# A two-layer transformer on one core: another way to combine the experts' rows, half a split moved from GpSimd to VectorE, and two modulation sums moved

## The chip, the cores and the metric

The kernel runs on one core of a Trainium2 chip. The metric is the device time of one execution in microseconds (us). The kernel before takes 2536.94 us, the median of three runs (2536.73 to 2538.14). For this kernel 0.2%, 5.07 us, is about what a measurement can tell from no change.

The engines by their short names: PE multiplies matrices, DVE is the vector engine, ACT the scalar engine, POOL is GpSimd. SP issues most DMAs (its queue is SPq); POOL also issues DMAs, among them the gathers by a list of row numbers.

## The reference

512 tokens of 1024 float32 columns pass two layers. In each, `h = x*(1+sc1)+sh1` goes through an attention block of two branches; its result is added to the scaled `x`, multiplied by a gate row, and normalised. Then `h = x*(1+sc2)+sh2` goes through a feed-forward block: dense in layer 0 (1024 to 2816 and back), eight experts in layer 1, of which each token uses the two that its router chose. The rows `sh`, `sc` and `g` are a vector-matrix product with `w_ada`, made once for each layer.

```python
mod = cond @ w_ada[l] + b_ada[l]
sh1, sc1, g1, sh2, sc2, g2 = jnp.split(mod[:, None, :], 6, axis=-1)
...
h = x * (1.0 + sc2) + sh2
f = _swiglu(...) if l % 2 == 0 else _moe(...)
x = _layernorm(DEEPNORM_ALPHA * x + g2 * f, ln2_g[l], ln2_b[l])
```

## The kernel before, in words

**Split products.** Every float32 operand is split into a rounded part (`wh`, `hTh`, by ACT) and the rest (`wl`, `hTl`, a subtraction on DVE or POOL), and each product is three matmuls: high by high, high by low, low by high (`mm3`, L127 to L129). A weight tile is loaded into `ws` by SP (L101), rounded by ACT (L111) and subtracted (L113). There are two `ws` buffers outside the expert stage.

**Order.** The program is written as one list. A planner puts the instructions of each engine in order: of those that its cost model holds ready, the first in the list goes first. On the chip each engine then runs its own list strictly in that order. `order(a, b)` keeps `a` behind `b` on one engine.

**The residual stage** (`residual`, twice with a following `early`): the last 512 columns of the product are finished for token tiles 0 to 3 in turn. DVE adds, takes statistics and normalises each tile (L945 to L947, L311 to L318, L980). After tile 2, `half_h(.., 0)` makes the modulated, turned `hTh` and `hTl` of tiles 0 and 1: for each pair of column blocks, four transposes into one PSUM tile `pt` (two buffers), DVE and ACT scale it into `hmod`, ACT rounds it to `hTh`, and for this half POOL makes all four subtractions `hTl` (L283). Then `early` (`early_ffn` after layer 0's attention, `early_first` after its feed-forward) loads its first weights and multiplies the first half by the column blocks 0 to 4, `half_h(.., 1)` makes the second half after tile 3 is normalised, and `early` goes on.

**The dense feed-forward loop** has 22 steps `f` of two products each. A generator `mod_steps` is resumed four times at the head of each step. For each of seven vectors it loads eight 512 KB pieces `mst` (two buffers), adds them up on DVE into `macc` (L213, L215), lets some resumptions pass (`wait`), sums over the partitions on PE (L222), copies (L225) and turns the result (L229), all with `order` behind the last product or weight split. The same loop writes zeros to the rows of `ybuf` that are kept for overflow, one DMA a step (L1077).

**The experts.** Each token has a place in two of eight slots (336, 320, 128, 128, 64, .. rows); `dst` holds the two row numbers, `gw` the two gates. Slots 0 and 1 run in the big lane, the others in the small lane beside it. A slot's output rows are stored to three buffers `ybuf`, of 512, 256 and 256 columns (`PIECES`). The big lane's last slot (slot 1) makes its output piece by piece: `out_turned`, `turn_back`, store. Then `Final.combine(i)` gathers for each of four token tiles the two rows of each token (eight gathers on POOL, L1681), adds them by their gates (L1683, DVE), and in the last piece normalises and writes the output (L311 to L318, L1689, L1691, L1692, L1694, L1695).

## Time and profile before

| | |
|---|---|
| median of three runs | 2536.94 us (2536.73 to 2538.14) |
| profiled execution, its own time | 2534.31 us |
| its span, first to last instruction | 2532.3 us |
| PE busy | 2431.6 us, 96% of the span |
| DVE, ACT, POOL busy | 70%, 57%, 17% |
| granted PE clock, mean | 0.986 |

Busy shares are averages over stages with different limits. The chain of work that ended last is followed back from the last instruction, at each step to what released it. A row of the time line gives the start, the length, the engine, the line of the kernel, the operation, the tiles written and read, the count of merged instructions, and in brackets the idle time ahead of it and what ended it.

### The profile page before, as it was taken

The numbers are of one execution on the slowest core, as the hardware profiler recorded it, in microseconds if no ns is written. First come the engines' busy times: TensorE is split into PE (matmuls) and PEld (weight loads), VectorE is DVE, ScalarE is ACT, GpSimd is POOL, SyncE is SP. The second block draws the span as 40 slices with busy tenths as digits, with TensorE's granted clock in tenths as the row PEclk, the third lists the DMA queues.
The fourth block names the chain that finished last, engine by engine and source line by source line (L and its number), as shares of the span: only waits on it lengthen the run. The fifth ranks groups of instructions, "written<-read, shape, count | busy, mean of one in ns | idle before, by whom it ended". The sixth has DMA issues, their size and how long they took to land.

```text
span 2532.3 us, 37049 instructions
## 1 busy us (share of the span) xinstructions
PE 2431.6 (96%) x13124; PEld 2077.9 (82%) x13124; DVE 1779.4 (70%) x2788; ACT 1432.8 (57%) x2320; POOL 430.8 (17%) x393
## 2 busy tenths in 40 slices
PE   8999999998999999999999997999999999999994
PEld 6878878787888888888877875888899998999994
DVE  3687876657666235787775356977788888888875
ACT  3577775224222215677763326676676777778761
POOL 1423330001000402333325004300000000000004
PEclk9999999999999999999999998999999999999997
DMA  8322226746866433222226329998999989999993
GB/s 236 90 62 64 75 76 193 220 148 210 273 212 211 150 100 109 78 63 76 73 73 192 100 76 285 316 327 274 318 319 296 320 285 319 333 302 332 293 333 122
DMA packets 453210, 502.20 MB, mean 198 GB/s; under 512 B 19314, under 2 KB 322920, under 8 KB 453016
## 3 DMA queue, kind: packets, MB, share of 16 engines
q1 hardware_dynamic: 437616, 453.64, 56.9%
q0 software_dynamic: 13888, 45.30, 5.1%
q8 instruction: 105, 1.72, 0.3%
q10 hardware_dynamic: 1512, 0.81, 0.1%
q14 instruction: 89, 0.73, 0.1%
HBM read 474.95 MB, written 24.74 MB: 197 GB/s over the span
## 4 chain that ended last, share of the span: by engine, by line
PE 80%; DVE 7%; ACT 4%; DMA 4%; issue 3%; POOL 1%; SPq 0%; ACTq 0%; DVEq 0%; POOLq 0%
PE ps L127 21%; PE ps L128 21%; PE ps L129 21%; PE ps L1373 5%; PE ps L1374 5%; PE pt L445 2%; DMA mst<-in_w_ada 1%; DVE wl L113 1%; PE ps L733 1%; PE ps L734 1%; ACT wh L111 1%; DVE ps L746 1%; ACT ps L742 1%; PE pt L1439 1%; PE ps L716 0%
## 5 line engine op out<-in xcount | busy, mean ns | idle before, releaser
L111 ACT ACTIVATE wh<-ws 128x1024 fp32r<-128x1024 f32 (+3 forms) x786 | 779.1, 1011 | 687.7 <-PE ps L128 343.4
L113 DVE TENSOR_TENSOR wl<-ws,wh 128x1024 fp32r<-128x1024 f32 (+3 forms) x712 | 837.3, 1195 | 365.2 <-ACT wh L111 357.1
L129 PE MATMUL ps<-hTh,wl 128*128 128x512 f32 (+1 forms) x904 | 346.9, 384 | 4.4 <-DVE wl L113 4.4
L127 PE MATMUL ps<-hTh,wh 128*128 128x512 f32 (+1 forms) x904 | 349.7, 387 | 0.1
L128 PE MATMUL ps<-hTl,wh 128*128 128x512 f32 (+1 forms) x904 | 348.7, 386 | 0.8 <-POOL hTl L283 0.8
L129 PE MATMUL ps<-x3h,wl 128*128 128x336 f32 (+1 forms) x704 | 220.5, 313 | 2.2 <-DVE wl L113 2.2
L127 PE MATMUL ps<-x3h,wh 128*128 128x336 f32 (+1 forms) x704 | 221.0, 314 | 0.0
L128 PE MATMUL ps<-x3l,wh 128*128 128x336 f32 (+1 forms) x704 | 219.9, 312 | 0.0
L113 POOL TENSOR_TENSOR wl<-ws,wh 128x1024 fp32r<-128x1024 f32 (+1 forms) x74 | 179.4, 2432 | 212.9 <-ACT wh L111 143.0
L129 PEld LDWEIGHTS ps<-hTh,wl 128*128 128x128 f32 x904 | 171.5, 190 | 36.9 <-DVE wl L113 5.3
L127 PEld LDWEIGHTS ps<-hTh,wh 128*128 128x128 f32 x904 | 171.6, 190 | 36.1 <-issue 3.7
L128 PEld LDWEIGHTS ps<-hTl,wh 128*128 128x128 f32 x904 | 171.4, 190 | 32.6 <-POOL hTl L283 2.1
L1373 PE MATMUL ps<-wh,xes 128*128 128x512 f32 (+1 forms) x384 | 143.3, 379 | 0.0
L1374 PE MATMUL ps<-wl,xes 128*128 128x512 f32 (+1 forms) x384 | 141.4, 374 | 0.0
L127 PEld LDWEIGHTS ps<-x3h,wh 128*128 128x128 f32 x704 | 132.2, 188 | 3.4
L128 PEld LDWEIGHTS ps<-x3l,wh 128*128 128x128 f32 x704 | 132.4, 188 | 3.0
L129 PEld LDWEIGHTS ps<-x3h,wl 128*128 128x128 f32 x704 | 132.1, 188 | 2.7 <-DVE wl L113 2.7
L127 PE MATMUL ps<-wh,hTh 128*128 128x256 f32 (+1 forms) x384 | 116.1, 304 | 1.8 <-DVE dq L520 1.0
L128 PE MATMUL ps<-wl,hTh 128*128 128x256 f32 (+1 forms) x384 | 113.6, 297 | 0.8 <-DVE wl L113 0.8
L129 PE MATMUL ps<-wh,hTl 128*128 128x256 f32 (+1 forms) x384 | 112.7, 295 | 0.0
L124 DVE TENSOR_TENSOR pTl<-pt,pTh 128x512 fp32r<-128x512 f32 x128 | 86.6, 686 | 36.0 <-ACT pTh L123 35.4
L128 PE MATMUL ps<-g3l,wh 128*128 128x336 f32 (+1 forms) x352 | 110.7, 315 | 0.0
(428 smaller groups left out, 5344.5 us busy)
## 6 DMA issues: line engine op xcount, KB each, us to landing
ws<-in_moe_w SPq DMA_DIRECT2D x492, 512.0 KB
ws<-in_w_in SPq DMA_DIRECT2D x94, 512.0 KB
mst<-in_w_ada SPq DMA_DIRECT2D x80, 512.0 KB
ws<-in_ffn_w SPq DMA_DIRECT2D x66, 512.0 KB
ws<-in_moe_w SPq DMA_DIRECT2D x48, 256.0 KB
wa<-in_w_ada SPq DMA_DIRECT2D x16, 512.0 KB
ws<-in_w_br_diff SPq DMA_DIRECT2D x16, 512.0 KB
ws<-in_w_out SPq DMA_DIRECT2D x16, 512.0 KB
```

The lines of the kernel that those rows point to most:

```text
L111: A.activation(h, st, AF.Copy)
L113: i = eng.tensor_tensor(l, st, h, op=OP.subtract)
L124: V.tensor_tensor(l, src, h, op=OP.subtract)
L127: T.matmul(o, ah, bh, start=start, stop=False)
L128: T.matmul(o, ah, bl, start=False, stop=False)
L129: last_mm[0] = T.matmul(o, al, bh, start=False, stop=stop)
L445: T.transpose(pt[:, t * P:(t + 1) * P], tiles[t][:, k * P:(k + 1) * P], ident)
L733: T.matmul(scs[m], q[:, m, tt], k[:, m], start=True, stop=False)
L734: last_mm[0] = T.matmul(scs[m], q[:, m, tt], kl[:, m], start=False, stop=True)
L742: A.activation(e, e, AF.Exp, scale=-1.0, bias=st[:, m:m + 1], accum_out=st[:, 2 + m:3 + m])
L1373: T.matmul(o, xs, wh, start=start, stop=False)
L1374: T.matmul(o, xs, wl, start=False, stop=stop)
```

## The change

Three edits. First, the last 512 columns (pieces 1 and 2). Before the last slot has stored anything there, 16 gathers fetch both rows of each token from `ybuf[1]` and `ybuf[2]`, where the last slot's rows hold zeros written earlier; `others` also works out for each token its row in the last slot (or a row of zeros) and its gate. At the end one row a token is gathered for each of the two pieces. Piece 0 is gathered as before; its adds are interleaved with the last products. Second, in the first half of the modulated input the last two of four subtractions are made from PSUM by DVE, after the second early weight is split. Third, the first two of seven modulation sums wait 7 and 4 resumptions where they waited 5 and 3, and the zeros go out two DMAs a step, 27 in all.

```diff
 def half_h(pool, xtiles, sc, sh, h, l, i, later=None):
+            if later is not None and k2 >= 4:
+                for j in range(2):
+                    k, pj = k2 + j, pt[:, j * 256:j * 256 + 256]
+                    if j == 0:
+                        last_split[0] = V.tensor_scalar(pj, pj, sc[:, k:k + 1], sh[:, k:k + 1], op0=OP.mult, op1=OP.add)
+                    else:
+                        A.activation(pj, pj, AF.Identity, scale=sc[:, k:k + 1], bias=sh[:, k:k + 1])
+                hk = h[:, k2:k2 + 2, tt]
+                mk = pt.rearrange("p (j c) -> p j c", j=2)
+                A.activation(hk, mk, AF.Copy)
+                later.append((l[:, k2:k2 + 2, tt], mk, hk))
+                continue
...
+    def small_parts(later):
+        for o, m, hk in later:
+            i = V.tensor_tensor(o, m, hk, op=OP.subtract)
+            order(i, last_split[0])
+        last_split[0] = i
...
-    zeros = [(y, SLOT_ROWS + i * P) for i in range(N_OVER) for y in ybuf]
+    zeros = [(y, SLOT_ROWS + i * P, P) for i in range(N_OVER) for y in ybuf]
+    zeros += [(y, SLOT[0] + i, min(P, SLOT[1] - i)) for i in range(0, SLOT[1], P) for y in ybuf[1:]]
...
-                 (5, 3, 2, 2, 2, 2, 2))
+                 (7, 4, 2, 2, 2, 2, 2))
...
-        for y, r in zeros[f:f + 1]:
-            SP.dma_start(y[r:r + P, :], zero[:, :y.shape[1]])
+        for y, r, m in zeros[2 * f:2 * f + 2]:
+            SP.dma_start(y[r:r + m, :], zero[:m, :y.shape[1]])
...
                     if nxt is None and i == 1:
                         for _ in gens[1]:
                             pass
-                    yield from out_turned(ew[2], g[1], part, c0, nc_, (FH, FT), False)
+                        fin.others(s)
+                    work = out_turned(ew[2], g[1], part, c0, nc_, (FH, FT), False)
+                    if nxt is None and i == 2:
+                        adds = fin.adds(0, fin.ys[0])
+                        for n in work:
+                            next(adds, None)
+                            yield n
+                        fin.after[0] = last_out[0]
+                        for _ in adds:
+                            pass
+                    else:
+                        yield from work
                     turn_back(part, SLOT[s], c0, nc_, row_stores(s))
-                    if nxt is None and i > 0:
-                        fin.combine(i - 1)
+                    if nxt is None and i == 1:
+                        fin.after[0] = last_out[0]
+                        for j in (1, 2):
+                            for _ in fin.adds(j, fin.ys[j]):
+                                pass
+                        fin.last_place(1)
...
+            late = [self.gathers(1, dst, (("xeh", 4), ("xel", 4))), self.gathers(2, dst, (("xg", 4), ("xg", 4)))]
+            self.ys = [self.gathers(0, dst, (("geh", 5), ("gel", 3)))] + late
...
+        def last_place(self, i):
+            tag = ("hs", "eg")[i - 1]
+            self.ys.append(self.gathers(i, self.row, ((tag, 2), (tag, 2))))
...
+        def end(self):
+            table = exp_table()
+            self.after[0] = last_out[0]
+            for _ in self.adds(1, self.ys[3], self.gate):
+                pass
+            self.last_place(2)
+            for t, _ in enumerate(self.adds(2, self.ys[4], self.gate)):
+                self.norm((t,), 3, table)
```

`early_ffn` calls `small_parts` between its second and third weight, `early_first` between its second and third. `adds` makes the gated adds of one piece, tile by tile, with the statistics; `norm` is the old end of `combine`. The branch for overflowing slots, which keeps the old way in `anew`, is not entered here.

## Rows read from the trace of the kernel before

**Rows 1.** The page: the chain that ended last, by engine.
```profile
PE 80%; DVE 7%; ACT 4%; DMA 4%; issue 3%; POOL 1%; SPq 0%; ACTq 0%; DVEq 0%; POOLq 0%
```

**Rows 2.** Time line of PE and POOL after the first residual.
```profile
583.14 0.58 PE L129 MATMUL ps<-hTh,wl 128*128 128x256 f32 x1 [3.55 <-DVE wl L113]
590.00 0.82 PE L266 MATMUL pt<-ident,u 128*128 128x128 f32 x6
...
579.50 2.49 POOL L283 TENSOR_TENSOR hTl<-hmod,hTh 128x512 fp32r<-128x512 f32 x2
```

**Rows 3.** Time line of DVE in the same stretch.
```profile
579.16 3.92 DVE L113 TENSOR_TENSOR wl<-ws,wh 128x1024 fp32r<-128x1024 f32 x1
584.33 1.21 DVE L113 TENSOR_TENSOR wl<-ws,wh 128x1024 fp32r<-128x1024 f32 x1
586.95 0.81 DVE L980 TENSOR_SCALAR u<-u,bmv 128x1024 f32<-128x1024 f32 x1
```

**Rows 4.** Windows: length, busy PE PEld DVE ACT POOL (count), PEclk, DMA share, GB/s.
```profile
583.00:588.50 5.50, 5.36 (x25) 5.37 (x26) 4.17 (x10) 0.50 (x2) 0.44 (x1) 0.51 0.75 224
588.50:603.00 14.50, 14.49 (x121) 14.13 (x121) 7.06 (x10) 7.07 (x13) 3.62 (x4) 1.00 0.30 88
603.00:619.60 16.60, 16.60 (x74) 13.24 (x72) 12.29 (x13) 6.19 (x9) 0.00 (x0) 1.00 0.93 288
619.60:626.00 6.40, 3.32 (x14) 1.97 (x14) 3.30 (x4) 1.06 (x1) 0.00 (x0) 0.73 0.67 208
965.00:970.00 5.00, 3.58 (x21) 3.35 (x22) 4.94 (x7) 0.60 (x3) 4.66 (x5) 1.00 0.48 159
```

**Rows 5.** Time line of PE and SPq in the feed-forward loop.
```profile
622.88 1.08 PE L222 MATMUL pt<-macc,ones 128*32 128x256 f32 x8 [3.08 <-DVE macc L215]
...
600.54 0.90 SPq L1077 DMA_DIRECT2D ybuf<-zero  x2
612.60 2.12 SPq L210 DMA_DIRECT2D mst<-in_w_ada  x2
```

**Rows 6.** Time line of DVE from the small lane's end to the last instruction.
```profile
2457.40 0.68 DVE L1502 TENSOR_TENSOR ye<-hs,g2row 64x512 f32<-64x512 f32 x1
2484.43 1.01 DVE L1527 SCALAR_TENSOR_TENSOR part<-ps,mcol,part 128x320 f32<-128x320 f32 x2 [4.12 <-PE ps L129]
2486.53 2.09 DVE L1683 SCALAR_TENSOR_TENSOR fu<-yg,r,fu 128x512 f32<-128x512 f32 x3 [0.44 <-DMA yg<-ybuf,r]
2495.81 0.99 DVE L1527 SCALAR_TENSOR_TENSOR part<-ps,mcol,part 128x320 f32<-128x320 f32 x2
2497.86 0.88 DVE L1683 SCALAR_TENSOR_TENSOR fu<-yg,r,fu 128x256 f32<-128x256 f32 x2 [0.67 <-DMA yg<-ybuf,r]
2506.84 0.49 DVE L1683 SCALAR_TENSOR_TENSOR fu<-yg,r,fu 128x256 f32<-128x256 f32 x1 [1.23 <-DMA yg<-ybuf,r]
2524.74 1.29 DVE L1694 SCALAR_TENSOR_TENSOR frows<-frows,bmv 128x1024 f32<-128x1024 f32 x1
```

**Rows 7.** Chain of waits at the end: start, length, what.
```profile
2487.58 4.31 DMA ybuf<-ye
```

**Rows 8.** Time line of POOL: first gather of piece 0, first of piece 2.
```profile
2479.53 1.65 POOL L1681 DMA_INDIRECT yg<-ybuf,r  x1 [22.98 <-DMA ybuf<-ye]
2503.80 1.18 POOL L1681 DMA_INDIRECT yg<-ybuf,r  x1 [1.44 <-issue]
```

**Rows 9.** One line's instructions: count, ns min/median/max, first and last start.
```profile
L1681 POOL DMA_INDIRECT yg<-ybuf,r x24: 943/949/1685, 2479.5 to 2513.5; - x24
```

**Rows 10.** The page: subtraction from PSUM, by DVE.
```profile
L124 DVE TENSOR_TENSOR pTl<-pt,pTh 128x512 fp32r<-128x512 f32 x128 | 86.6, 686 | 36.0 <-ACT pTh L123 35.4
```

**Rows 11.** Time line of DVE and PE after the second residual.
```profile
965.49 1.77 DVE L946 SCALAR_TENSOR_TENSOR u<-u,ftmp 128x512 f32<-128x512 f32 x1
968.73 1.11 DVE L473 TENSOR_SCALAR dgc<-cols 128x8 f32<-128x8 f32 x1
972.02 0.87 PE L266 MATMUL pt<-ident,u 128*128 128x128 f32 x6 [0.41 <-DVE u L980]
```

More of the change, by code (lines that the diff above doesn't have):

```diff
@@ L256, in gate_row, with half_h @@
         return row_tile(pool, "grow", modrow[i:i + 1], "grow")
-    def half_h(pool, xtiles, sc, sh, h, l, i):
+    def half_h(pool, xtiles, sc, sh, h, l, i, later=None):
         tt = slice(i * 256, i * 256 + 256)
@@ L939, in residual @@
         sts = [pool.tile([P, 3, 6], F32, name=nm("bst"), tag="bst", bufs=4) for _ in range(NT)]
+        later = []
         def fin(pz, t, i, c0, n):
@@ L986, in residual @@
                         l = hp.tile([P, KT, S], F32R, name=nm("hTl"), tag="hTl")
-                        half_h(pool, us, *ab, h, l, 0)
+                        half_h(pool, us, *ab, h, l, 0, later)
         if ab is None:
@@ L991, in residual @@
         behind[0] = None
-        e = early(h, l)
+        e = early(h, l, later)
         if EARLY_POOL:
@@ L1014, in build, with early_ffn @@
     ahead_of = {}
-    def early_ffn(h, l):
-        ws = [(f, w, wload([P, KT, P], kview(I[w][0], 0, KT, f * P, P)), psum())
-              for f, w in ((0, "ffn_w1"), (0, "ffn_w3"), (1, "ffn_w1"))]
+    def small_parts(later):
[3 more added lines that the diff above has]
+        last_split[0] = i
+    def early_ffn(h, l, later):
+        ws = []
+        for i, (f, w) in enumerate(((0, "ffn_w1"), (0, "ffn_w3"), (1, "ffn_w1"))):
+            if i == 2:
+                small_parts(later)
+            ws.append((f, w, wload([P, KT, P], kview(I[w][0], 0, KT, f * P, P)), psum()))
         for i, tt in enumerate(halves_of):
@@ L1027, in early_ffn, with early_first @@
         yield
-    def early_first(h, l):
+    def early_first(h, l, later):
         w_in = I["w_in"][1]
@@ L1032, in early_first @@
         pz = [psum() for _ in range(NT)]
+        small_parts(later)
         lat = [wload([P, 2, LAT], kview(w_in, 0, 2, 0, LAT))]
@@ new lines, in gathers @@
+        def gathers(self, i, idx, tags):
+            n = PIECES[i][1]
+            ys = []
+            for tag, k in tags:
+                y = xp.tile([P, k, n], F32, name=nm("yg"), tag=tag, bufs={"xg": XG, "hs": 3, "eg": 2}.get(tag, 1))
+                ys += [y[:, j, :] for j in range(k)]
+            m = idx.shape[2]
+            for t in range(NT):
+                for k in range(m):
+                    G.indirect_dma_start(out=ys[m * t + k], out_offset=None, in_=ybuf[i],
+                                         in_offset=bass.IndirectOffsetOnAxis(ap=idx[:, t, k:k + 1], axis=0))
+            return ys
@@ new lines, in others @@
+        def others(self, s):
+            r, n = starts[s], SLOT[s]
+            here, lt = et([P, NT, 2]), et([P, NT, 2])
+            V.tensor_scalar(here, dstf, r - 0.5, None, op0=OP.is_gt)
+            V.tensor_scalar(lt, dstf, r + n - 0.5, None, op0=OP.is_lt)
+            V.tensor_tensor(here, here, lt, op=OP.mult)
+            V.tensor_scalar(lt, dstf, float(SLOT_ROWS), None, op0=OP.subtract)
+            V.tensor_tensor(lt, lt, here, op=OP.mult)
+            rowf = et([P, NT])
+            V.tensor_reduce(rowf, lt, axis=AX.X, op=OP.add)
+            V.tensor_scalar(rowf, rowf, float(SLOT_ROWS), None, op0=OP.add)
+            self.row = et([P, NT, 1], I32)
+            V.tensor_copy(self.row, rowf.unsqueeze(2))
+            V.tensor_tensor(lt, here, gw.rearrange("p k t -> p t k"), op=OP.mult)
+            self.gate = et([P, 1, NT])
+            V.tensor_reduce(self.gate.rearrange("p o t -> p (o t)"), lt, axis=AX.X, op=OP.add)
+            self.after = [None]
+            late = [self.gathers(1, dst, (("xeh", 4), ("xel", 4))), self.gathers(2, dst, (("xg", 4), ("xg", 4)))]
+            self.ys = [self.gathers(0, dst, (("geh", 5), ("gel", 3)))] + late
@@ new lines, in adds @@
+        def adds(self, i, ys, gate=None):
+            c0, n = PIECES[i]
+            for t in range(NT):
+                uc = self.us[t][:, c0:c0 + n]
+                for k in range(len(ys) // NT):
+                    j = V.scalar_tensor_tensor(uc, ys[len(ys) // NT * t + k], (gw if gate is None else gate)[:, k, t:t + 1],
+                                               uc, op0=OP.mult, op1=OP.add)
+                    if self.after[0] is not None:
+                        order(j, self.after[0])
+                if i == 0 or gate is not None:
+                    V.bn_stats(self.sts[t][:, i, :], uc)
+                yield
@@ new lines, in last_place, with norm @@
+        def last_place(self, i):
+            tag = ("hs", "eg")[i - 1]
+            self.ys.append(self.gathers(i, self.row, ((tag, 2), (tag, 2))))
+        def norm(self, ts, n, table):
+            for t in ts:
+                u = self.us[t]
+                mean, r = ln_stat(xp, self.sts[t][:, :n], table)
+                V.scalar_tensor_tensor(u, u, mean, self.lg, op0=OP.subtract, op1=OP.mult)
+                if t < 2:
+                    A.activation(u, u, AF.Copy, scale=r)
+                    G.tensor_tensor(u, u, self.lb, op=OP.add)
+                else:
+                    V.scalar_tensor_tensor(u, u, r, self.lb, op0=OP.mult, op1=OP.add)
+                SP.dma_start(out[0, t * P:(t + 1) * P, :], u)
@@ new lines, in end, with anew @@
+        def end(self):
[6 more added lines that the diff above has]
+                self.norm((t,), 3, table)
+        def anew(self):
+            table = exp_table()
+            self.after = [None]
+            for i, tags in enumerate(((("geh", 5), ("gel", 3)), (("xeh", 4), ("xel", 4)), (("xg", 4), ("xg", 4)))):
+                for t, _ in enumerate(self.adds(i, self.gathers(i, dst, tags))):
+                    if i > 0:
+                        V.bn_stats(self.sts[t][:, i, :], self.us[t][:, PIECES[i][0]:PIECES[i][0] + PIECES[i][1]])
+                    if i == 2:
+                        self.norm((t,), 3, table)
@@ L1716, in build @@
         done[i] = 9.0 if n is None else done[i] + n / share[i]
-    fin.combine(len(PIECES) - 1)
+    fin.end()
     behind[0] = last_mm[0] = None
@@ L1740, in build @@
         again.prepare()
-        for i in range(len(PIECES)):
-            again.combine(i)
+        again.anew()
     ms.close()
```

26 lines of the change are left out of this document (removed).

## The prediction

> **What bounds the kernel now.** I read the chain of waits first: PE has 80% of it, DVE 7% [rows 1]. So the kernel is a row of matmuls, and an edit pays where PE stands still, runs slowly, or has nothing left to do. I then read the time lines and windows at the places that the edits touch.
>
> After the first residual PE stops for 3.55 us, ended by a `wl` on DVE [rows 2]. That subtraction took 3.92 us; its like five microseconds later took 1.21 [rows 3]. Beside it stands POOL with two `hTl` subtractions from 579.50 on [rows 2], so POOL holds DVE up for 2.7 us. [...] The 25 matmuls of the slow window took 5.36 us where 121 instructions took 14.49 at full clock, 0.12 each: 25 x 0.12 = 3.0, so the clock cost 2.4.
>
> In the feed-forward loop PE waits 3.08 us for the first modulation sum, whose last piece lands late [rows 5]; DMA is 0.93 busy in the 16.6 us before it, and the clock in the window behind it is 0.73 [rows 4].
>
> At the end PE's last product lets DVE write `part` at 2495.81 [rows 6]. Everything after that is tail: stores that land in 4.31 us [rows 7], eight gathers on POOL, the first at 2503.80 [rows 8], the last at 2513.5 [rows 9], gated adds and normalisation on DVE from 2506.84 to 2526.03 [rows 6], the output's DMA to 2532.3.
>
> **The change part by part.**
>
> *Half the split on DVE, first residual.* Two of POOL's four subtractions go, the pair that starts at 579.50. The second `wl` then takes 1.21 instead of 3.92: 2.7 us gained on DVE. DVE gets two subtractions from PSUM, 0.69 each [rows 10]: 1.4 us, queued ahead of the third early weight and, as I take it, of tile 3's normalisation. ACT's rounding now waits for DVE and ACT to have scaled both halves in PSUM, but it makes one copy of two blocks instead of two passes; I cost it at nothing because DVE is late by more. PE resumes at 579.16 + 1.21 = 580.4 instead of 583.14. After the stop it needs 30 matmuls of 0.12 up to the transposes of the second half at 590.00; the third `wl` is ready at 585.5 - 2.7 + 1.4 = 584.2, so PE waits again, some 1.9 us, and is through at 586.0. The transposes need tile 3's row, normalised at 586.95 + 0.81 = 587.76 before [rows 3], so at 586.5 after. They start 3.5 us earlier than at 590.00, and what is behind them follows. **-3.5**, bounds -5.0 (PE never waits again and tile 3 is put ahead: the stop shortened by 2.7 and the clock's 2.4) and -1.1 (the second wait drops the clock as the first one did). The PSUM tiles are held until the subtraction; the next user of the two buffers is the second half's transposes, which come later anyway.
>
> *The same edit, second residual.* Here the clock stayed at 1.00 [rows 4] and the transposes at 972.02 wait for tile 3 [rows 11]. DVE's L946 took 1.77 and L473 1.11 beside POOL, where L946's kind takes 0.7 and eight elements next to nothing: some 2.0 us back, less 1.4 for the subtractions from PSUM. **-0.6**, bounds -2.0 and +1.4.
>
> *Modulation sums.* A step resumes the generator four times. The first sum moves from the 14th resumption to the 16th; both are in step 3, ahead of its products and behind those of step 2. PE meets it at the same place, so I give the wait no gain. The second moves from step 6 to 7, the others by three resumptions. The seven need 91 resumptions, the loop gives 88: the last sum runs after the loop, at the same instructions, with at most one short wait of PE for a copy. 0, bounds -4.0 (the wait of 3.08 goes, and 0.27 of the 3.32 busy microseconds at clock 0.73, 0.9 [rows 4, 5]) and +0.5.
>
> *Zeros.* 27 instead of 21, two a step. Before, SP issued the zeros of steps 0 to 2 before the last two pieces `mst` of the first sum [rows 5]. With two a step three more go ahead of them, one of 256 KB and two of 128 KB (the tiles are 128 x 512 and 128 x 256 floats). At the 288 GB/s of that window [rows 4] 512 KB take **+1.8**. The pieces land that much later, and PE's wait grows with them. Bounds 0 (the planner leaves them behind the loads) and +7.4 (below).
>
> *The tail.* The 16 gathers of pieces 1 and 2 need the small lane's last store: its row is made by 2458.08 [rows 6], lands 4.3 later [rows 7], so POOL starts at about 2463.2. A gather costs POOL 0.95 [rows 9] and 0.30 of idle time behind it, 1.25 in all, (2513.5 - 2503.8) / 7 = 1.39 where long ones are among them: the 16 end at 2483.2, piece 0's eight, before from 2479.53, at 2493.2, four more for piece 1 at 2498.2. All are done before 2503.80, when piece 2's stores have landed. Then four gathers run instead of eight: POOL is done 5.0 us earlier. DVE takes over as the bound of the tail: from 2506.84 to 2526.03 it loses four adds of 0.44 [rows 6], 1.8 us, and the first gathers come 1.25 apart where an add takes 0.49, so it idled 0.76 at each of three; I count half of these 2.3 as filled: 3.0 gained. Against it: DVE now makes the 16 adds, 16 x 0.44 = 7.0, and the first two steps of piece 0, four adds of 0.70 and two statistics taken to be as long, 4.2, between the two `part` groups: 2485.44 + 11.2 = 2496.6 instead of 2495.81, 0.8 late, on the path. The remaining two steps and piece 1's four last adds fit between there and 2506.84. `others` is some ten small operations on DVE while it waits for products. **-2.2**, bounds -5.0 (POOL's whole saving) and +1.8 (below).
>
> The 16 gathers now run beside DVE's weight subtractions. Of the 24 before, one started beside a `wl` and took 1.65 us [rows 8]; the median is 0.95, and 20 of the 24 took no more than 0.98 [rows 9], those beside DVE's adds among them. [...]
>
> *Sum:* -3.5 - 0.6 + 0 + 1.8 - 2.2 = -4.5. The profiled execution took 2534.31, 2.0 over its span, and would take 2529.8. It lies 2.6 under the median of the runs; I take the difference to the median: 2536.9 - 4.5 = **2532.4**.
>
> **The rivals.**
> 1. *Zeros crowd the loads out* (slower than before). Ten zeros, 1.8 MB, went out before 650; two a step make it twenty, 3.4 MB. The 1.7 MB more take 5.8 us at 288 GB/s, and one more drop to the lower clock as at 619.6 costs about 1.6. For it: DMA 0.93 busy there. Against it: beyond the one wait PE had none in that stretch. It decides from an extra wait above 6.3, which eats all three gains: -6.3 + 7.4 = +1.1, 2538.0.
> 2. *Piece 2's `part` waits behind all of piece 0's adds.* If the planner puts all four steps ahead, 7.0 + 8.4 end at 2500.8, 5.0 late; the tail then loses 2.0 instead of gaining 2.2: 2536.6. For it: order is fixed by a model's times; against it: `part` stands ahead of step three in the list.
> 3. *The second wait after the first residual drops the clock.* +2.4: 2534.8. Against it: gaps of under a microsecond at 965 to 970 left it at 1.00 [rows 4]; a wait of 1.9 is between the two cases.
> 4. *The early gathers come late.* With 0.7 more each (1.65 against 0.95) the 16 end at 2494.4, piece 0's at 2504.4, piece 1's at 2509.4, the last four at 2514.4, as before: no gain in the tail, 2534.6. For it: the one long row beside a `wl`; against it: the 20 short ones. [...]
> 5. *The first sum moves behind step 3's first product*, because the zeros make it late in the planner's model too: its wait goes, 2532.4 - 1.8 - 4.0 = 2526.6.
>
> **How the numbers follow.** Forecast 0.42, rivals in order 0.13, 0.12, 0.10, 0.10, 0.13. Faster by over 0.2% means below 2531.9, slower above 2542.0; 0.2% is what a measurement of this kernel can tell. The forecast with its own 1.5 either way lies half below that bound; rival 5 is below it; rivals 3 and 4 reach it seldom. Faster 0.21 + 0.13 + 0.05, and a little for the planner's order elsewhere: 0.43. Slower: a third of rival 1, and the same allowance: 0.10. Same 0.47. The range goes from rival 5's time to just under rival 1's: 2526.6 to 2537.6, leaving out half of rival 5 and most of rival 1.
>
> **What would show it.** Right: the stop before the second `wl` under 1.2 us and no window near 0.5 behind it; two PSUM subtractions of 0.69 behind that `wl`; the transposes of the second half some 3.5 us sooner after it; the wait before the first L222 about 5 us; the early gathers near 2463, last gathers four, and DVE's last instruction some 27.2 us after piece 2's `part` starts (30.2 before). Wrong: a third stop of PE in that early stage, POOL gathers of 1.6 us and more in a row, piece 2's `part` later than half a microsecond behind its last product, or a loss in the stages between, which no edit touches.

## The result and the profile after

The kernel after takes 2555.34 us, the median of four runs (2549.07 to 2556.65); the kernel before 2537.36 beside it (four runs, 2536.73 to 2538.14). The ratio is 1.0079 with a 95% interval of 1.0066 to 1.0092: 18.0 us slower, where 4.5 us faster was forecast. The profiled execution of after took 2556.65, its span 2554.9, its mean granted clock 0.983.

Where the 22 us between the two profiled executions arise is seen from PE. Both run the same 13124 matmuls, and the table gives how much later the matmul of the same number starts than in before, at seven times of before's trace (us; minus is sooner). The runs e1 to e18 are told below. It is one execution each: the profiled one of e2 lies 7.0 over the median of its runs, that of e11 9.1 under, so a difference of a few us in one cell can be chance.

| | 570 | 600 | 640 | 941 | 990 | 1498 | 2480 |
|---|---|---|---|---|---|---|---|
| after | +0.3 | -3.1 | -2.9 | -2.9 | +0.1 | +2.9 | +4.1 |
| e9, after word for word | -0.3 | -3.7 | -3.8 | -3.9 | -1.8 | -1.0 | +0.6 |
| e1, the tail edit alone | +2.2 | +1.3 | +0.9 | +2.6 | +2.6 | +4.1 | +4.0 |
| e12, the half split alone | 0.0 | -2.4 | -3.5 | -3.6 | -2.3 | -0.7 | +1.6 |
| e17, half split and sums | +0.8 | -1.7 | -4.0 | -4.1 | -1.2 | -0.1 | +1.9 |

The first residual (570 to 600) gains 3.4 in after and the second (941 to 990) loses 3.0. Between 990 and 2480, which no edit touches, every kernel of the table drifts up by 1.4 to 4.0 against this one execution of before, which was itself 2.6 under its median. What is left comes behind 2480: 22.3 - 4.1 = 18.

The chain of waits by engine, on the page of after, hardly differs from [rows 1]; a stop of 17 us is under 1% of it. A view by shares doesn't show this loss.

```profile
PE 81%; DVE 7%; ACT 4%; DMA 4%; issue 3%; POOL 1%; SPq 0%; ACTq 0%; DVEq 0%; POOLq 0%
```

The time line of DVE in after, from the first residual to the end (start, length, instruction, in brackets the idle time and what ended it; "issue" means that the engine waited for nothing that the profile shows, "remote" that the profile does not tell what ended the wait). Here and below the rows are a choice; those between them are left out:

```profile
574.87 2.32 DVE L113 TENSOR_TENSOR wl<-ws,wh 128x1024 fp32r<-128x1024 f32 x1
580.05 1.21 DVE L113 TENSOR_TENSOR wl<-ws,wh 128x1024 fp32r<-128x1024 f32 x1
581.79 0.68 DVE L1032 TENSOR_TENSOR hTl<-pt,hTh 128x512 fp32r<-128x512 f32 x1
582.99 0.67 DVE L1032 TENSOR_TENSOR hTl<-pt,hTh 128x512 fp32r<-128x512 f32 x1
...
966.84 0.28 DVE L329 TENSOR_SCALAR bmv<-bmv 128x1 f32<-128x1 f32 x1
970.05 0.29 DVE L476 TENSOR_TENSOR lv<-lv 128x128 f32<-128x128 f32 x1 [2.94 <-DMA lv<-in_lambda_k]
970.26 0.15 DVE L330 TENSOR_SCALAR bmv<-bmv 128x1 f32<-128x1 f32 x1
...
2483.46 0.96 DVE L113 TENSOR_TENSOR wl<-ws,wh 128x768 fp32r<-128x768 f32 x1 [3.69 <-PE ps L128]
2505.76 0.55 DVE L1553 SCALAR_TENSOR_TENSOR part<-ps,mcol,part 128x320 f32<-128x320 f32 x1 [21.34 <-remote]
2520.43 1.01 DVE L1553 SCALAR_TENSOR_TENSOR part<-ps,mcol,part 128x320 f32<-128x320 f32 x2 [1.83 <-issue]
2543.18 3.36 DVE L1772 SCALAR_TENSOR_TENSOR fu<-fu,bmv,frows 128x1024 f32<-128x1024 f32 x1
2547.14 1.28 DVE L1772 SCALAR_TENSOR_TENSOR frows<-frows,bmv 128x1024 f32<-128x1024 f32 x1
```

Against [rows 3] and [rows 6]: the second `wl` takes 1.21 instead of 3.92, and two subtractions from PSUM of 0.68 stand behind it. Near 970 a product of L476 waits for a load, ahead of the rest of tile 3's normalisation. In the tail DVE waits 21.34 us for piece 1's product. The time lines of PE and of POOL in after:

```profile
581.32 0.39 PE L129 MATMUL ps<-hTh,wl 128*128 128x256 f32 x1 [1.71 <-DVE wl L113]
587.22 0.82 PE L267 MATMUL pt<-ident,u 128*128 128x128 f32 x6
606.59 0.50 PE L129 MATMUL ps<-hTh,wl 128*128 128x512 f32 x1 [0.59 <-DVE wl L113]
614.19 0.50 PE L127 MATMUL ps<-hTh,wh 128*128 128x512 f32 x1 [2.31 <-ACT wh L111]
615.45 0.50 PE L129 MATMUL ps<-hTh,wl 128*128 128x512 f32 x1 [0.52 <-DVE wl L113]
622.27 0.64 PE L222 MATMUL pt<-macc,ones 128*32 128x256 f32 x8
...
2488.84 0.31 PE L128 MATMUL ps<-g3l,wh 128*128 128x320 f32 x1
2506.46 0.66 PE L1561 MATMUL pt<-ident,part 128*128 128x128 f32 x2 [17.32 <-issue]
...
2473.63 1.00 POOL L1718 DMA_INDIRECT yg<-ybuf,r  x1 [12.94 <-DVE wl L113]
2488.42 0.95 POOL L1718 DMA_INDIRECT yg<-ybuf,r  x1 [0.30 <-issue]
2503.45 0.94 POOL L1718 DMA_INDIRECT yg<-ybuf,r  x1 [0.30 <-issue]
```

Compare [rows 2] and [rows 8]. The transposes start at 587.22 instead of 590.00. In the loop the wait of 3.08 before L222 [rows 5] is gone and three waits for weights, 3.42 together, have come. From 2488.84 on PE stands still for 17.3 us, and this is the loss. Meanwhile POOL goes on with a row of 24 gathers that began at 2473.63; the 12th starts at 2488.42, the 24th ends at 2504.39. DVE goes on 1.4 us later, PE 2.1. The windows of after (length, busy PE PEld DVE ACT POOL with counts, PEclk, DMA share, GB/s):

```profile
583.00:588.50 5.50, 5.50 (x49) 5.50 (x49) 4.08 (x11) 0.67 (x3) 0.55 (x1) 1.00 1.03 342
970.00:975.00 5.00, 3.37 (x17) 3.37 (x17) 2.80 (x9) 2.05 (x6) 0.55 (x1) 0.66 0.30 120
2490.00:2495.00 5.00, 0.00 (x0) 0.00 (x0) 0.00 (x0) 0.00 (x0) 3.78 (x5) 0.87 0.38 105
2495.00:2500.00 5.00, 0.00 (x0) 0.00 (x0) 0.00 (x0) 0.00 (x0) 3.78 (x5) 0.50 0.65 175
```

The first is the window that was at clock 0.51 with 25 matmuls [rows 4]: now 1.00 and 49. The second lies behind the second residual; it is told further down. In the other two all engines but POOL are idle, and the granted clock falls to 0.50; it stayed there until 2514.2, so that piece 2's `part` came 14.7 us behind piece 1's, where before had 11.4 [rows 6].

The tail in sum, profiled executions: +4.1 up to 2480, +17.2 for the stop (2505.76 - 2484.43 - 4.1), +3.3 between the two `part`, and 28.0 from piece 2's `part` to DVE's last instruction where before had 30.2, -2.2. DVE ends 22.4 us later.

### The profile page after: what moved, and what is told of

Same layout as the page of the kernel before. It is cut to its first block, busy times and chain, and to the rows that moved or that the text cites. A ratio compares the mean times of both kernels' runs of the same rounds, so it can differ in the third digit from the quotient of the medians.

```text
span 2554.9 us, 37083 instructions
## 1 busy us (share of the span) xinstructions
PE 2436.7 (95%) x13124; PEld 2081.2 (81%) x13124; DVE 1778.8 (70%) x2810; ACT 1434.1 (56%) x2316; POOL 435.7 (17%) x397
## 2 busy tenths in 40 slices
DMA packets 454331, 503.91 MB, mean 197 GB/s; under 512 B 19539, under 2 KB 323785, under 8 KB 454137
## 4 chain that ended last, share of the span: by engine, by line
PE 81%; DVE 7%; ACT 4%; DMA 4%; issue 3%; POOL 1%; SPq 0%; ACTq 0%; DVEq 0%; POOLq 0%
PE ps L127 21%; PE ps L128 21%; PE ps L129 21%; PE ps L1399 5%; PE ps L1400 5%; PE pt L458 2%; PE ps L746 1%; PE ps L747 1%; ACT wh L111 1%; DMA ws<-in_moe_w 1%; DVE wl L113 1%; ACT ps L755 1%; DVE ps L759 1%; PE pt L1465 1%; PE ps L729 0%
## 5 line engine op out<-in xcount | busy, mean ns | idle before, releaser
L129 PEld LDWEIGHTS ps<-hTh,wl 128*128 128x128 f32 x904 | 170.9, 189 | 37.7 <-DVE wl L113 5.8
```

The costliest lines, as they stand in the source:

```text
L129: last_mm[0] = T.matmul(o, al, bh, start=False, stop=stop)
```

## The experiments

Runs of one group share a chip and the runs of the kernel before; the groups (e1 to e4, e5 to e8, e9 to e12, e13 to e15, e16 to e18) ran on five different chips, which turned out to matter; on which chip the result was taken is not on record. Diffs are against the kernel after where nothing else is said.

**e1: the tail edit alone.**
```diff
-                        half_h(pool, us, *ab, h, l, 0, later)
+                        half_h(pool, us, *ab, h, l, 0)
...
-                 (7, 4, 2, 2, 2, 2, 2))
+                 (5, 3, 2, 2, 2, 2, 2))
```


> The kernel before with the combine alone changed (and the zero rows that it needs); the split of the first half and the modulation steps stay as before. Theory G (in the kernel after, TensorE and VectorE stand still from 2489.15 to 2506.46 because of the unbroken row of 24 gathers on GpSimd, which ends at 2504.39): the stop of about 17 us is here too, its end 1 to 2 us behind the last gather of the row; time 2552 to 2558 us. Rival F (part of the loss comes from the edits in the front, whose stretches ended 4 us late at 2460 in the kernel after): the stop is here, but the tail starts 4 us earlier, time about 2549 to 2552. Rival D (the stop needs both parts of the change): no stop, 2535 to 2540.

Measured: 2556.67 against 2535.86, ratio 1.0074 (1.0056 to 1.0092). The stop is there: DVE's `part` comes at 2508.14 after 22.19 us. The tail edit alone, with the zeros that it needs, makes the loss.

**e2: the half split and the modulation sums alone** (before's combine and before's zeros, one a step).
```diff
+            if later is not None and k2 >= 4:
...
-                 (5, 3, 2, 2, 2, 2, 2))
+                 (7, 4, 2, 2, 2, 2, 2))
```
The diff is against before.

> The kernel before with the split of the first half from PSUM and the modulation steps (7, 4); the combine and its zeros as before. Theory G: no stop in the tail, the first residual 3.2 us sooner as in the kernel after, the second residual gives 3 us back where VectorE waits 2.94 us for the load of lambda; time 2534 to 2538. Rival F: the front edits cost 4 us at 2460, time 2540 to 2543.

Measured: 2531.11, ratio 0.9976 (0.9967 to 0.9986), 4.7 us faster, no stop.

**e3: without the 16 early gathers.** They are left out, and the adds read the rows of piece 0 in their place, so the output differs.
```diff
-            late = [self.gathers(1, dst, ...), self.gathers(2, dst, ...)]
-            self.ys = [self.gathers(0, dst, (("geh", 5), ("gel", 3)))] + late
+            y0 = self.gathers(0, dst, (("geh", 5), ("gel", 3)))
+            self.ys = [y0] + [[y[:, :PIECES[i][1]] for y in y0] for i in (1, 2)]
```


> The kernel after without the 16 early gathers of pieces 1 and 2 (their 16 additions read the gathered rows of piece 0 instead, so that the output is another); 8 gathers stand in a row in place of 24. Theory G: no stop of PE in the middle of piece 1; 17 to 20 us less than the kernel after, 2535 to 2539. Rival W (VectorE waits there for a semaphore that has nothing to do with the gathers, or the order by the planner does it): the stop of over 10 us stays, over 2548.

Measured: 2536.59, ratio 1.0001 (0.9990 to 1.0012). Piece 1's `part` is on time, so the stop belongs to the early gathers; piece 2's is late all the same, by 5.4 us. DVE's two groups in e3:

```profile
2484.09 1.01 DVE L1553 SCALAR_TENSOR_TENSOR part<-ps,mcol,part 128x320 f32<-128x320 f32 x2 [4.03 <-PE ps L129]
2500.64 0.99 DVE L1553 SCALAR_TENSOR_TENSOR part<-ps,mcol,part 128x320 f32<-128x320 f32 x2
```

**e4: the early gathers of piece 2 behind piece 1's products**, meant to shorten the row to 16.
```diff
+                        fin.last_place(1)
+                        fin.ys[2] = fin.gathers(2, dst, (("xg", 4), ("xg", 4)))
```


> The kernel after with the 8 early gathers of piece 2 moved behind the 4 of piece 1's last place, so that 16 gathers stand in a row in place of 24, and piece 2's additions of other places' rows behind piece 1's last place. Theory G: the stop ends 1 to 2 us behind the row's last gather, about 2496, so 7 us or less in place of 17.3, or it is gone as in the kernel before, which has 8 and 8 with a gap of 2.6 us; the tail then ends 10 to 17 us sooner, time 2538 to 2547. Rival W: the stop stays at 17 us, time 2553 or more.

Measured: 2553.65, ratio 1.0062 (1.0042 to 1.0081). The edit missed its aim: the planner put the eight back into the row, 24 from 2471.14 to 2502.17. PE stops for 19.39 us. It says nothing of a row of 16.

**e5: before's combine with 16 gathers that nobody uses**, and the zeros that they need. The diff is against before.
```diff
+                        fin.unused()   # 16 gathers of pieces 1 and 2, ahead of piece 1's product
```


> The kernel before, with its own combine, and beside it 16 early gathers of pieces 1 and 2 at the place where the kernel after has them, into tiles that nothing reads (and the zero rows that they need). Theory G (a long unbroken row of gathers on GpSimd is what stops TensorE and VectorE): 24 gathers in a row, a stop of 10 to 20 us in piece 1 behind the last matmul, though VectorE's order is the one of before; time 2548 to 2560. Rival W (the new order of VectorE's additions makes the stop): no stop; at most 16 x 1.25 us of GpSimd ahead of piece 0's gathers, time 2535 to 2545.

Measured: 2543.15 against 2533.51, ratio 1.0041 (1.0027 to 1.0056). No stop, although 32 gathers stand in one row; instead the gathers that are used come late, and piece 2's `part` waits in DVE's queue behind adds that wait for them, while PE waits 10.82 us. DVE in e5:

```profile
2483.09 1.01 DVE L1529 SCALAR_TENSOR_TENSOR part<-ps,mcol,part 128x320 f32<-128x320 f32 x2 [4.12 <-PE ps L129]
2504.32 0.99 DVE L1529 SCALAR_TENSOR_TENSOR part<-ps,mcol,part 128x320 f32<-128x320 f32 x2
```

**e6: one row a token in piece 2 alone**; piece 1 as before.
```diff
-            late = [self.gathers(1, dst, ...), self.gathers(2, dst, ...)]
+            late = [None, self.gathers(2, dst, (("xg", 4), ("xg", 4)))]
```


> The kernel after with early gathers for piece 2 alone; piece 1 is combined as before (8 gathers behind its stores). 16 gathers stand in a row in place of 24. Theory G, by the length of the row: the row ends about 10 us sooner (about 2494 in place of 2504), so the stop is 7 us or less, time 2535 to 2545; if a row of 16 is short enough, none, 2529 to 2535. Rival W: the stop stays at 15 us or more, time over 2550.

Measured: 2534.01, ratio 1.0003 (0.9991 to 1.0014), no stop: half of the edit, and no gain. Its gathers stand in one row of 28, so this isn't a test of 16 either. Piece 2's `part` comes on time: DVE waits 0.51 for its product.

**e7: a GpSimd fill ahead of every fourth early gather**, to break the row; **e8: piece 0's gathers ahead of the other 16.**
```diff
+                    if m == 2 and self.paced and (m * t + k) % 4 == 0:
+                        for _ in range(1024 // n):
+                            z = G.memset(ys[m * t + k], 0.0)
```
```diff
+            self.ys = [self.gathers(0, dst, (("geh", 5), ("gel", 3)))]
+            self.ys += [self.gathers(1, dst, ...), self.gathers(2, dst, ...)]
...
+                    elif m == 2 and self.last0 is not None:
+                        order(g1, self.last0)
```


> The kernel after with fills of the gathers' own tiles set between its gathers on GpSimd (24 fills of 128x256 or 128x512, about 0.5 to 0.9 us each by the rows of other fills), so that the same gathers come further apart and end some 15 us later. Theory G, if it is the rate of gathers that counts: TensorE goes on through piece 1 with stops under 3 us. If it is that any gather is under way: the stop lasts until the later end of the row, over 25 us. Rival W: a stop of about 17 us as before.

> The kernel after with piece 0's 8 gathers ahead of the 16 early ones. They wait for piece 0's stores, so the row of 24 starts some 7 us later (about 2480) and ends about 2511. Theory G: the stop begins at the same matmul or later and ends later with the row, 2511 to 2515. Rival W (what ends the stop is tied to the product, not to the row): VectorE's first part of piece 1 stays within 2 us of 2506.

Measured: e7 2543.43 in one run, e8 2552.12 in one run, neither with the stop. But e5 has none on this chip either, and the kernel after was not run there, so as tests of the stop both are inconclusive. In e7 PE waits 9.71 us for piece 2's `part`, in e8 13.69: in both it stands in DVE's queue behind adds that wait for gathers.

**e9: the kernel after, word for word; e10: e5 once more; e11: all 24 early adds behind the last `part`; e12: the half split alone** (before with the first hunk).
```diff
-                        adds = fin.adds(0, fin.ys[0])
-                        for n in work:
-                            next(adds, None)
-                            yield n
+                    yield from work
...
+            for j in (0, 1, 2):
+                for _ in self.adds(j, self.ys[j]):
+                    pass
             for _ in self.adds(1, self.ys[3], self.gate):
```
The diff is that of e11.

> The kernel after, word for word, beside the others of this group. The stop stood in all three kernels of the first groups whose combine is the one of after with 24 gathers in a row at full rate (after, e1, e4) and in none of the next group (e5 to e8), among them e5 with 40 gathers in a row. Theory R (the row at full rate together with the new combine makes the stop): the stop of 15 to 20 us is here again, 2549 to 2557 us. Rival C (it was the chip or the session on which those kernels ran): no stop of over 5 us in piece 1, time 2535 to 2546 us, and this kernel then behaves as e7.

> The kernel before with the 16 early gathers that nothing reads, once more, on the same chip as the kernel after. Theory R: no stop in piece 1, as in e5, and 2541 to 2546 us, while e9 has it. Rival C: both have the stop or neither; with a stop it comes to 2550 or more.

> The kernel after with all 24 additions of other places' rows behind piece 2's last part on VectorE, so that VectorE waits for no gather while TensorE works. Theory R in the form 'VectorE's waits for gathers hold the hand-over': no stop in piece 1, piece 2's part within 1 us of its product, and the 24 additions (some 13 us) then lie behind it: 2533 to 2542. Rival 'the row of gathers alone': the stop in piece 1 stays at 15 to 20 us, 2550 or more.

> The kernel before with the split of the first half from PSUM alone: zeros, modulation steps and combine as before. If the 4.75 us that e2 gained come from the split, as the terms A and B of the prediction have it (4.1 us), the same here: 2528 to 2532 beside 2533 to 2537 for before. Rival (the modulation steps (7, 4) bring part of it): 2 us or less of gain.

Measured against 2534.64: e9 2537.9, ratio 1.0011 (0.9996 to 1.0025), without the stop. With e18 below, where the same program has it, this makes the stop a matter of the chip as well as of the kernel. e10 2545.95, 1.0036 (1.0024 to 1.0048). e11 2543.18, 1.0029 (1.0015 to 1.0044): its `part` comes at once, but the adds then lengthen the end: from the end of piece 2's product to DVE's last instruction 37.7 us in its profiled execution, 34.6 in e9, 30.5 in before. That execution, 2534.1, is the fastest of its ten, so the trace shows this part of the loss and not the whole. e12 2531.72, 0.9985 (0.9969 to 1.0000).

e9 shows what the tail edit costs without the stop. DVE, PE and POOL in e9:

```profile
2484.93 1.01 DVE L1553 SCALAR_TENSOR_TENSOR part<-ps,mcol,part 128x320 f32<-128x320 f32 x2 [4.03 <-PE ps L129]
2498.48 2.26 DVE L1750 SCALAR_TENSOR_TENSOR fu<-yg,r,fu 128x512 f32<-128x512 f32 x3 [2.15 <-DMA yg<-ybuf,r]
2501.85 0.99 DVE L1553 SCALAR_TENSOR_TENSOR part<-ps,mcol,part 128x320 f32<-128x320 f32 x2
2521.02 2.31 DVE L331 TENSOR_TENSOR bmv<-bmv 128x1 f32<-128x1 f32 x1
2525.42 3.36 DVE L1772 SCALAR_TENSOR_TENSOR fu<-fu,bmv,frows 128x1024 f32<-128x1024 f32 x1
2529.38 1.28 DVE L1772 SCALAR_TENSOR_TENSOR frows<-frows,bmv 128x1024 f32<-128x1024 f32 x1
...
2502.54 1.09 PE L1561 MATMUL pt<-ident,part 128*128 128x128 f32 x4 [6.49 <-DVE part L1553]
...
2470.02 1.00 POOL L1718 DMA_INDIRECT yg<-ybuf,r  x1 [12.87 <-DVE wl L113]
2472.61 1.82 POOL L1718 DMA_INDIRECT yg<-ybuf,r  x1 [0.31 <-issue]
2520.40 2.92 POOL L1770 TENSOR_TENSOR fu<-fu,frows 128x1024 f32<-128x1024 f32 x1 [5.75 <-ACT fu L1769]
2524.59 3.11 POOL L1770 TENSOR_TENSOR fu<-fu,frows 128x1024 f32<-128x1024 f32 x1 [1.28 <-ACT fu L1769]
```

Piece 2's product ends at 2496.0; its `part` stands in DVE's queue behind piece 0's adds, and these wait for gathers until 2498.48: 5.8 us on the path. The first gather starts at 2470.02, not at 2463. It waits for the last store of the small lane, whose row is made by 2458.7 and which goes out as two DMAs, at 2458.7 and 2459.2. The row names a `wl` of DVE as what ended the wait, but where the traces have the landing (e1, e5, e9, e13, e16) the first gather starts 0.60 to 0.64 behind the second store's, and 0.39 to 1.21 behind that `wl`. How long the store takes is said by the last line of the answer on its tile in e9 (us from issue to landing):

```profile
L1570 SPq DMA_DIRECT2D ybuf<-ye x2: 472/534/595, 2458.7 to 2459.2; - x2
DMA to landing us min/median/max: 10.2/10.3/10.5
```

In e1, e5, e13 and e16 it is 10.7 to 11.3. Five weight loads go out on the same queue just ahead of it, and the DMA engines are full while it is under way (share 0.9 or more from 2465 to 2467.3 in e9, 1.04 from 2460 to 2465 in before); that this is the reason is likely and not shown.

**e13, e14, e15: the kernels of e9, e5 and e6 once more, on a fourth chip.**

> The kernel after, word for word, on one more chip. Theory C (the stop of about 17 us in piece 1 belongs to some chips: those of the result and of e1 and e4 have it, that of e9 doesn't): either about 2550 to 2557 with the stop, or about 2535 to 2541 without; which one is not foreseen, and the two kernels beside it tell what sets it off on this chip.

> The kernel before with 16 early gathers that nothing reads, beside e13. If e13 has the stop: theory G (a long row of gathers is enough on such a chip) expects a stop of over 10 us in piece 1 here too, 2555 or more; the rival (it needs the new combine) none, 2541 to 2547. If e13 has none, none here.

> The kernel after with early gathers for piece 2 alone (16 in a row), beside e13. If e13 has the stop: theory G by the length of the row expects none or one that ends by 2497 (7 us or less). If e13 has none, none here and 2530 to 2538.

Measured against 2534.87: e13 2540.48, ratio 1.0018 (1.0004 to 1.0032), no stop; e14 2545.2 and e15 2531.3 in one run each, no stop. The tests with 28 and 32 gathers in a row thus ran only on chips where nothing stopped.

**e16: piece 0's adds behind piece 2's last `part`; e17: e2 once more; e18: the kernel after.** e16 is e11's diff with `self.adds(0, self.ys[0])` alone moved.

> The kernel after with piece 0's 8 additions and their statistics behind piece 2's last part on VectorE; the 16 early additions stay ahead of it. Theory P (where TensorE doesn't stop in piece 1, what the new combine loses is piece 2's part, which comes 5.8 us behind its product in e9 because it stands behind piece 0's additions and these wait for gathers): the part comes within 1 us of the product, TensorE's 6.5 us wait is gone, and 3 to 6 us come back against e18: ratio to before 0.997 to 1.000. Rival E (the end of VectorE's chain is what counts; the additions are only moved behind the part): within 1.5 us of e18. With the stop in piece 1 on this chip both stand some 17 us higher.

> The kernel before with the split of the first half from PSUM and the modulation steps (7, 4) and the combine of before, once more, on the chip of e16 and e18: ratio to before 0.9965 to 0.999, as in e2 (0.9976); the lowest of the three kernels of this group by theory P and rival E alike.

> The kernel after, word for word, beside e16 and e17. Without the stop in piece 1 a ratio to before of 1.000 to 1.003 as in e9 and e13, with piece 2's part over 4 us behind its product; with the stop 1.006 to 1.009 as in the result.

Measured against 2534.61: e16 2554.49, ratio 1.0075 (1.0053 to 1.0097); e17 2533.33, 0.9995 (0.9984 to 1.0006); e18 2555.36, 1.0080 (1.0064 to 1.0097). This chip has the stop, in e16 and e18. What e16's order would gain could not be seen under it; at the end it costs little, 28.6 us from piece 2's `part` to DVE's last instruction against 28.4 in e18. But e16 shows the stop best, because PE still had matmuls of piece 1 to do. PE, ACT and POOL in e16, and the same instruction of ACT in e9:

```profile
2483.37 0.31 PE L128 MATMUL ps<-g3l,wh 128*128 128x320 f32 x1
2483.53 0.31 PE L129 MATMUL ps<-g3h,wl 128*128 128x320 f32 x1
2483.87 0.31 PE L127 MATMUL ps<-g3h,wh 128*128 128x320 f32 x1
2484.61 0.39 PE L128 MATMUL ps<-g3l,wh 128*128 128x320 f32 x1 [0.43 <-issue]
2485.30 0.31 PE L129 MATMUL ps<-g3h,wl 128*128 128x320 f32 x1 [0.30 <-issue]
2486.71 0.42 PE L127 MATMUL ps<-g3h,wh 128*128 128x320 f32 x1 [1.10 <-issue]
2493.78 0.43 PE L128 MATMUL ps<-g3l,wh 128*128 128x320 f32 x1 [1.66 <-issue]
2505.93 0.66 PE L1561 MATMUL pt<-ident,part 128*128 128x128 f32 x2 [11.71 <-DVE part L1553]
...
2482.49 0.85 ACT L111 ACTIVATE wh<-ws 128x768 fp32r<-128x768 f32 x1 [5.23 <-remote]
...
2483.89 0.95 POOL L1709 DMA_INDIRECT yg<-ybuf,r  x1 [0.30 <-issue]
```

```profile
2479.07 0.85 ACT L111 ACTIVATE wh<-ws 128x768 fp32r<-128x768 f32 x1 [2.06 <-PE ps L128]
```

Until 2483.53 a matmul starts every 0.15 us. Then, as the 11th gather of the row starts at 2483.89, PE goes on one matmul at a time with pauses of 0.3 to 1.7 us that no instruction of another engine ends. So it isn't only the hand-over from PE to DVE that is late: PE itself is held. None of its matmuls is missing from the trace: all have 13124. The same irregular starts are in e1 (from 2487.89, between the 11th gather at 2487.08 and the 12th) and in e18 (from 2488.30, the 11th at 2488.27); in after PE's last matmul starts at 2488.84, the 12th gather at 2488.42, and in e4 at 2486.46 and 2486.22. In all five DVE's `part` comes 1.4 to 3.9 us after the row's last gather has ended. The kernels with rows of eight ahead of piece 1's end (before, e2, e3, e17) show none of it on the same chips.

What comes late is PE's signal. The traces record the updates of each semaphore, the counters by which one engine releases another. In before the product's last matmul ends at 2484.39, PE's semaphore is updated at 2484.40 and `part` starts at 2484.43. In after that matmul ends at 2488.41, the update comes at 2505.74, 17.3 us later, and `part` at 2505.76; in e16 the three are 2489.79, 2505.20 and 2505.23. The rest of PE's stop is its wait for `part`.

The first sign is earlier than PE's own pauses. ACT's last rounding stands idle 2.05 to 2.09 us for PE's semaphore in after and in the fifteen traces without the stop, but 2.88 in e4, 3.67 in e1, 3.71 in e18 and 5.23 in e16 (where the update comes at 2482.47), while the 7th to 9th gather run and PE still starts a matmul every 0.15 us. So PE's signals are late first, and its own starts after them.

## Why the prediction was wrong

**The tail, -2.2 forecast, is the step that failed, in two ways.**

*A stop that no step held.* "All are done before 2503.80" failed by little: the 24th gather ends at 2504.39 in after and the 28th at 2508.32 in e9. But on the chips of the result, of e1 to e4 and of e16 to e18 a row of 24 gathers holds up PE's signals, in four of five traces from the 7th to 9th on, and PE itself from the 11th or 12th: 17.2 us in after, and the lower clock behind it. I had priced the gathers by POOL's time alone, from rows of eight, and at nothing for PE; [rows 8, 9] hold no long row beside matmuls. That it is the row of gathers is shown by e3 (none without the 16) and by e1 (tail alone); that it is not the row alone is shown by e9 and e13, the same kernel without a stop, and by 32 in a row in e5. Undoing the first residual's edit or moving piece 0's adds doesn't take it away (e1, e16).

*Rivals 2 and 4, together.* "Lands 4.3 later [rows 7], so POOL starts at about 2463.2" took the landing of the big lane's store for that of the small lane's, which takes 10.3 (and 2458.08 + 4.3 is 2462.4, not 2463.2). The gathers start 6.8 us late in e9, the 24th ends at 2502.82 where the sum had 2493.2, and piece 0's adds stand in front of piece 2's `part` waiting for it: 5.8 us against my 0.8. Rival 2 had the place right and its price, 2536.6, near e9's 2537.9, but rested on the number of adds; e9's adds wait for rows. Rival 4 had the gathers late, but by long rows: two of the 32 in e9 take 1.82 and 1.68, one 1.35, the median is 0.95. The three make 2.0 us together; with some of 1.0 to 1.2 the row of 24 is 2.8 longer than in the sum. The one of 1.82, at 2472.61, starts beside a `wl` of 2472.39 to 2473.62, that of 1.68, at 2490.24, beside adds of 2489.03 to 2491.09; but the gather at 2479.87, with a `wl` of 2479.95 to 2480.91 beside it, takes 0.94. So single gathers were long beside DVE, not the row. e11 shows that the adds can't simply go elsewhere: behind `part` they make the way from product to end 3.1 longer than in e9. With eight early adds instead of sixteen (e6, e15) `part` was on time.

*The end: right in direction, too large in size.* From piece 2's `part` to DVE's last instruction 28.8 us in e9 and 28.0 in after; 27.2 forecast, 30.2 before. Of the 3.0 that I had counted 1.4 and 2.2 came.

**The first residual, -3.5 forecast: the mechanism right, the size at its upper end.** -3.4 by the table. The fifteen traces with this edit measure 1.8 to 3.8 for the stretch, half of them 2.4 or less, and the four without it 0.1 to 0.8, so the edit itself is worth less than 3.5. The stop before the second `wl` is 1.71, not under 1.2, because the first `wl` takes 2.32 where it took 1.22: it starts at 574.87, just behind one of POOL's other subtractions (574.82), while in before it started just ahead of them (574.48 and 574.50), and the first of them took 2.34 where the second took 1.28. The transposes start 587.22 where 586.5 was forecast, the window that was at clock 0.51 [rows 4] is at 1.00, and the two subtractions take 0.68 as forecast. Rival 3 did not come.

**The second residual, -0.6 forecast: wrong in sign, +3.0.** The planner moved the product L476 ahead of L330. DVE reaches it at 967.1 and waits 2.94 for `lv`, with tile 3's normalisation behind it; in before the same product stands behind that normalisation, at 971.88, and waits for nothing. In e3 the wait is 0.91, and the stretch measures -0.4. PE's wait for the transposes grows from 0.41 to 2.58, and behind it the granted clock is 0.66 from 970 to 975, where before had 1.00. The other traces bear the cause out: of the fifteen with the half split, the three where DVE waits under 1 us for this load measure -0.4 to -0.9, the twelve where it waits 2.0 to 3.1 measure +1.2 to +3.2. The size of the subtractions was right; what my bounds (+1.4) lacked is a load that DVE now reaches too early.

**Modulation sums 0 and zeros +1.8: wrong in the mechanism.** The stretch measures +0.2 in after and -0.1 in e9. The wait before the first L222, forecast to grow from 3.08 to about 5, is gone in every kernel with two zeros a step, with the moved sums or without them (e1, e5), and stays in those with before's zeros: 2.56 in e12, and in e17, which has the moved sums,

```profile
620.66 0.64 PE L222 MATMUL pt<-macc,ones 128*32 128x256 f32 x8 [2.17 <-DVE macc L215]
```

So it goes with the zeros. With them SP issues three zeros in a row ahead of loads, and PE waits for a weight instead, 2.31 at 614.19 in after and 1.49 in e1. PE meets the first sum at the same matmul in all kernels. That is rival 1's mechanism at less than its price, and rival 5's gain (no wait) without the order that it supposed. How long the stretch takes follows the granted clock more than either edit: its mean is 1.00 in e12, e17 and e5, which has two zeros a step and before's sums, and they gain 1.2, 2.3 and 2.2; it is 0.96 in before, after, e9 and e1. So no run gives the sums or the zeros a price of their own.

In all, of the 22.3 us between the profiled executions the start has 0.3, the front edits -0.2 (-2.3 forecast), the drift 4.0 and the tail 18.2 (-2.2 forecast). Where the kernel doesn't stop (e9) the tail still loses about 4: 5.5 more between the two `part`, 1.4 less behind the second. The best that was measured is the front without the tail edit and with before's zeros: e2 0.9976, e17 0.9995, the half split alone 0.9985. None of the three measures slower than before, and none has an interval wholly beyond 0.2%.

What stays open: why a long row holds PE and its signals on some chips. Whether 16 in a row would do it there was not tried. Whether the row without the new combine would do it there (e5's kernel) was not tried either. Before's own later row of 16 has a pause after eight; e2's has none, on a chip with the stop, and nothing stops. But PE has no products left by then, so neither tells.

## What to carry to other kernels

Price a moved DMA by the landing of the very transfer that it waits for, at its own time: 10.3 and 4.3 us were two stores of one kernel in one tail. An instruction that waits for data should not stand ahead of one on the critical path in the same engine's queue (5.8 us for piece 2's `part` in e9); count what is queued behind each added wait. Before a kernel is judged by a few runs of a per cent, it is worth running it on a second chip: here one and the same program is 0.1% or 0.8% slower.

## What the hardware showed that I had not expected

The traces with the stop also lack records. Each gather here is ended by 16 records of semaphore updates of POOL's queue; 24 gathers make 384. Records counted in the trace:

```text
                       gathers from-to     records   of    PE held
before                 2480 to 2520            212   384   no
e17                    2480 to 2520             81   384   no
after, the row of 24   2470 to 2510            123   384   yes
e18, the row of 24     2470 to 2510            113   384   yes
e12                    2480 to 2520            384   384   no
e9                     2470 to 2520            512   512   no
```

The view of the DMA issues shows it as a landing time that is missing (after) or there (e9, the last number, us):

```profile
yg<-ybuf,r POOLq DMA_INDIRECT x32
```

```profile
yg<-ybuf,r POOLq DMA_INDIRECT x32, 3.5
```

The packets themselves are all there, 454331 on the page of after and 454330 on that of e9. The other traces follow: e1 to e4 and e16 lack records of the gathers at the end, e5 to e8, e10, e11 and e13 to e15 have all of them. So the two go together by chip: on the chips where records get lost, the row of 24 ahead of piece 1's end holds PE (17.2 us in after); where none are lost, no row does. Which of the two makes the other, or whether something else makes both, is not shown, and no run here was taken without records. So it is open whether the stop belongs to the recording or to the kernel.

In four places GpSimd held a DVE instruction for the rest of its own. Beside the two `tensor_tensor` of 2.92 and 3.11 at 2520.40 and 2524.59 in e9 a DVE operation on one element a partition (L331) takes 2.31 instead of 0.16, and one of 1024 elements 3.36 instead of 1.28. The 3.92 of [rows 3] and the 2.32 of the first `wl` in after are the same. In all four DVE ends, within 0.2 us, when it would have ended had it started with the end of GpSimd's instruction: 2523.33 beside 2523.32 + 0.16, 2528.78 beside 2527.70 + 1.28, 583.08 beside 581.99 + 1.21, 577.19 beside 576.11 + 1.22. So in these four the price of the meeting is what GpSimd has left to do.
